# The order of all engines taken from a simulation with queues, with another opening of the first FFN

## The chip, the cores and the metric

The kernel runs on one core of one Trainium2 chip. The metric is the device time of one execution in microseconds (us). The kernel before takes 2179.03 us (median of 3 runs, 2178.09 to 2179.07). A core has TensorE (PE) for matmuls, VectorE (DVE), ScalarE (ACT) and GpSimd (POOL), and SyncE (SP), which here only issues transfers. Each engine executes its own list of instructions in order and waits on semaphores for the others.

## The reference, cut to what matters

528 tokens (16 meta tokens and 512 of the input) of 1024 channels go through two layers, each an FFN, a mixer and an FFN:

```python
def swiglu(x, w_gate, w_up, w_down):
    return (jax.nn.silu(x @ w_gate) * (x @ w_up)) @ w_down
...
def mixer(z, w_in, gla_w2, gla_b2, gla_gn, q_norm, k_norm, w_pa, w_pb, b_merge, w_out, cos, sin):
    h = z @ w_in
    (q_a, k_a, v_a, r_a, lr_f, lr_b, q_b, k_b, v_b, g_a, g_b) = jnp.split(h, SPLIT_POINTS, axis=-1)
    a = gla_branch(q_a, k_a, v_a, r_a, lr_f, lr_b, gla_w2, gla_b2, gla_gn)
    b = attention_branch(q_b, k_b, v_b, q_norm, k_norm, cos, sin)
    y = (jax.nn.sigmoid(g_a + b_merge[0]) * (a @ w_pa)
         + jax.nn.sigmoid(g_b + b_merge[1]) * (b @ w_pb))
    return y @ w_out
...
    for l in range(DEPTH):
        h = h + 0.5 * swiglu(rmsnorm(h, norm_gains[l, 0]),
                             ffn_w_gate[l, 0], ffn_w_up[l, 0], ffn_w_down[l, 0])
        h = h + mixer(rmsnorm(h, norm_gains[l, 1]), w_in[l], gla_w2[l], gla_b2[l], gla_gn[l],
                      q_norm[l], k_norm[l], w_pa[l], w_pb[l], b_merge[l], w_out[l], cos, sin)
        h = h + 0.5 * swiglu(rmsnorm(h, norm_gains[l, 2]),
                             ffn_w_gate[l, 1], ffn_w_up[l, 1], ffn_w_down[l, 1])
```

All is float32. The attention has 8 query heads of 64 on 2 key heads and runs in blocks of 128 queries.

## The kernel before, in words

Activations lie with channels on the 128 partitions and tokens along the free axis; `h` holds all eight chunks of 128 channels. Every float32 product is made of three matmuls on operands that are split into a high part (a cast, on ACT: L337 for weights, tile `whi`) and a low part (a subtraction, on DVE: L338, tile `wlo`): high by high, high by low, low by high.

**FFN.** The weights come in slabs of 128 x 1024. The products run in a scheme with seven products of half blocks instead of eight, so sums of weight blocks are needed besides the blocks. They are made by `begin_sums` and `sums`: by transfers that add into a tile (issued on POOL's queue, L255), by a negation on ACT (L250) or by a subtraction on DVE (L300). `ffn_steps` lists an FFN's steps in the order of the program: `P` is one of the seven products of a pair of FFN chunks, `S` one of the down products, `D` a plain down product, `H` the hidden values. The first FFN of the program (f = (0, 0)) opens with plain products (`G`, `F`, by `whole_matmuls`, L744), because the weights arrive while it runs; `Q` squares `h`, `R` makes the means over the channels (L523) and the reciprocal roots, and `X` makes the differences of halves of `h` that the seven products use (`differences`, L589 on ACT and L592 to L595 on DVE) and their split parts (`parts_of`, L601, L602). `early` and `late` with `direct` (L559, L560) make the split chunks of `h` that the plain products read. The loop at the end of `build` runs them with the weight pieces (L244, L245). The odd chunks' second halves come by the transfer at L1474.

**Mixer.** `project` (L517) makes one projection of 128 channels: 24 matmuls per half of the tokens. After the gated linear attention (`gla_pair`), `attention` runs over units of two blocks of 128 queries of one head: `probs` makes the scores (L1222, L1223), their maximum (DVE L1225, L1230), the exponential (ACT L496 with the read of its accumulator), the reciprocal (DVE L1232) and scales the row (ACT L1234 for the first block of a unit, DVE L1236 for the second). `weighted` transposes the probabilities (L1247, L1257), splits them (ACT L1250 and L1260, DVE L1251 and L1261) and multiplies them with the values (L1263 to L1265); the sum of both parts goes to tile `e` (ACT L1270, DVE L1271). The scores lie in tile `ss` (two buffers of two PSUM banks), transposes and weighted values in `sm` (two buffers), projections in `mm` (two buffers). The projections of the merge gates are written in part ahead of the attention and in part behind it (`gate_pairs`); what comes before what on an engine is not the order of the program alone.

**What sets the order.** The program is a list of instructions with dependencies through tiles. The scheduler of the tile framework puts them in an order for each engine, by a simulation of its own and by priorities: the program's order, `tc.high_priority()`, and `tc.issue_after(x)`, which lets an instruction become ready only behind x. On the chip each engine follows its list; a matmul that waits holds up every matmul behind it.

## Time and profile before

| | |
|---|---|
| median of 3 runs | 2179.03 us (2178.09 to 2179.07) |
| profiled execution | 2179.76 us |
| its span, first to last instruction | 2178.0 us |
| granted TensorE clock, mean | 0.998 |
| PE busy | 2152.3 us, 99% |
| DVE busy | 1795.3 us, 82% |
| ACT busy | 1238.8 us, 57% |
| POOL busy | 113.8 us, 5% |
| share of the chain that ended last | PE 81%, DVE 12%, ACT 4%, issue 2%, DMA 1% |

In the rows that the prediction shows, `<-` stands between what an instruction writes and what it reads; `xc` are operands of an FFN, `x` of the mixer, `t` scratch tiles, `q` split probabilities, `sc` scalars of a softmax row, `g` gates and FFN operands. A row of the waits has the engine, tile and line that waited, what it waited for, and the total, the times and the longest in us. A row of the groups has, behind the bar, busy us and mean ns of one instruction, then the idle us before it and what ended them. A row of the timeline has start, duration, and in brackets the idle time before it. In the rows of windows each engine has its busy us and its instructions; then come the granted clock, the DMA share and GB/s.

### The profile page before, as it was taken

To read this page: it belongs to the slowest core of one execution; us is meant where nothing else is said; L and a number is where in the kernel's file an instruction comes from. 1 tells how busy PE (TensorE), PEld (TensorE's weight loads), DVE (VectorE), ACT (ScalarE), POOL (GpSimd) and SP (SyncE) were. 2 spreads that over 40 slices of the span, in tenths; PEclk is the share of its full clock that TensorE was granted. 3 is DMA by queue.
4 is the path that set the end of the run, shared out by engine and by line. 5 is a ranking of instruction groups with operands and counts; after the bars stand their busy time and mean duration, and the time that the engine had idled before them with its cause. 6 is when DMAs were issued, how large, how long until landed. Compare 5 with 4: busy or idle time off the path is not lost.

```text
span 2178.0 us, 40250 instructions
## 1 busy us (share of the span) xinstructions
PE 2152.3 (99%) x16496; PEld 2062.5 (95%) x16496; DVE 1795.3 (82%) x2748; ACT 1238.8 (57%) x1839; POOL 113.8 (5%) x135
## 2 busy tenths in 40 slices
PE   9999999999999999999999999999999999999998
PEld 9999999989999999999999999988788888999997
DVE  7987979777976689888799879797779767997986
ACT  7645557455784556464575455574557836554544
POOL 1100000000000000010010000000000001000100
PEclk9999999999999999999999999999999999999999
DMA  7866755112113557675567667552121146775751
GB/s 219 214 178 184 211 153 143 67 59 69 49 40 126 136 169 190 194 189 179 173 164 188 195 182 204 152 138 97 49 78 50 49 136 157 201 202 177 199 160 68
DMA packets 90999, 315.08 MB, mean 145 GB/s; under 512 B 10048, under 2 KB 14016, under 8 KB 90816
## 3 DMA queue, kind: packets, MB, share of 16 engines
q1 hardware_dynamic: 70656, 244.87, 32.7%
q0 software_dynamic: 18608, 65.54, 16.9%
q8 instruction: 130, 2.13, 0.4%
q10 hardware_dynamic: 1552, 2.11, 0.3%
q14 instruction: 53, 0.43, 0.1%
HBM read 291.51 MB, written 2.10 MB: 135 GB/s over the span
## 4 chain that ended last, share of the span: by engine, by line
PE 81%; DVE 12%; ACT 4%; issue 2%; DMA 1%; ACTq 0%; DVEq 0%
PE ss L694 36%; PE mm L517 14%; PE ss L845 13%; PE ss L517 7%; DVE wlo L338 3%; PE sm L517 2%; DVE h L853 1%; DMA w<-win 1%; PE sm L1247 1%; PE ss L744 1%; DVE g L806 1%; PE ss L1222 1%; PE ss L523 1%; ACT t L496 1%; PE sm L1263 1%
## 5 line engine op out<-in xcount | busy, mean ns | idle before, releaser
L694 PE MATMUL ss<-xc,whi 128*128 128x264 f32 (+1 forms) x4704 | 858.1, 284 | 2.3 <-DVE g L781 1.0
L694 PEld LDWEIGHTS ss<-xc,whi 128*128 128x128 f32 x4704 | 726.8, 188 | 4.0 <-DVE g L781 1.2
L694 PE MATMUL ss<-xc,wlo 128*128 128x264 f32 (+1 forms) x2352 | 666.0, 283 | 1.2 <-DVE wlo L338 1.2
L338 DVE TENSOR_TENSOR wlo<-w,whi 128x1024 fp32r<-128x1024 f32 (+1 forms) x350 | 419.7, 1205 | 64.0 <-ACT whi L337 63.6
L337 ACT CAST whi<-w 128x1024 fp32r<-128x1024 f32 (+1 forms) x350 | 358.0, 1038 | 167.3 <-PE ss L694 75.5
L694 PEld LDWEIGHTS ss<-xc,wlo 128*128 128x128 f32 x2352 | 442.9, 188 | 1.8 <-DVE wlo L338 1.8
L517 PE MATMUL mm<-x,whi 128*128 128x264 f32 (+1 forms) x1712 | 385.0, 315 | 0.0
L517 PEld LDWEIGHTS mm<-x,whi 128*128 128x128 f32 x1712 | 277.8, 188 | 16.0 <-issue 1.0
L845 PE MATMUL ss<-g,whi 128*128 128x264 f32 (+1 forms) x1520 | 284.0, 285 | 4.0 <-DVE h L853 1.7
L517 PE MATMUL mm<-x,wlo 128*128 128x264 f32 (+1 forms) x856 | 265.9, 315 | 0.0
L845 PEld LDWEIGHTS ss<-g,whi 128*128 128x128 f32 x1520 | 236.1, 188 | 8.1 <-DVE g L806 4.2
L845 PE MATMUL ss<-g,wlo 128*128 128x264 f32 (+1 forms) x760 | 214.9, 283 | 0.0
L698 ACT COPY c<-ss 128x528 f32<-128x528 f32 (+1 forms) x126 | 75.0, 595 | 224.0 <-PE ss L694 223.8
L337 ACT CAST whi<-raw 128x1024 fp32r<-128x1024 f32 x114 | 119.3, 1048 | 129.2 <-PE mm L517 93.5
L338 DVE TENSOR_TENSOR wlo<-raw,whi 128x1024 fp32r<-128x1024 f32 x114 | 139.2, 1222 | 56.1 <-ACT whi L337 52.2
L517 PEld LDWEIGHTS mm<-x,wlo 128*128 128x128 f32 x856 | 159.5, 188 | 8.1 <-issue 0.5
L845 PEld LDWEIGHTS ss<-g,wlo 128*128 128x128 f32 x760 | 142.9, 188 | 0.0
L255 POOL DMA_DIRECT2D w<-win x62 | 54.4, 877 | 1475.7 <-DVE wlo L338 510.0
L496 ACT ACTIVATE c<-c 128x528 f32<-128x528 f32 (+1 forms) x88 | 56.4, 642 | 108.3 <-DVE c L771 108.2
L845 PE MATMUL ss<-c,whi 128*128 128x264 f32 (+1 forms) x608 | 115.8, 286 | 1.5 <-ACT c L803 0.7
L338 DVE TENSOR_TENSOR wlo<-s,whi 128x1024 fp32r<-128x1024 f32 (+1 forms) x90 | 107.5, 1196 | 0.9 <-ACT whi L337 0.8
L517 PE MATMUL ss<-g,whi 128*128 128x264 f32 (+2 forms) x516 | 103.7, 310 | 0.0
(295 smaller groups left out, 3536.3 us busy)
## 6 DMA issues: line engine op xcount, KB each, us to landing
w<-win SPq DMA_DIRECT2D x330, 512.0 KB, 4.3
raw<-wts SPq DMA_DIRECT2D x114, 512.0 KB, 3.3
w<-win POOLq DMA_DIRECT2D x58, 512.0 KB, 7.5
s<-win POOLq DMA_DIRECT2D x24, 512.0 KB, 7.6
w<-s POOLq DMA_DIRECT2D x24, 512.0 KB, 5.4
w<-win SPq DMA_DIRECT2D x20, 384.0 KB, 3.9
s<-w POOLq DMA_DIRECT2D x6, 512.0 KB, 8.8
h<-xt SPq DMA_DIRECT2D x3, 528.0 KB, 8.0
```

What stands on the lines that cost most here:

```text
L255: return self.nc.gpsimd.dma_start(t, src, accum_op=ALU.add)
L337: self.cast = nc.scalar.copy(hi[:, :n], w[:, :n]).ins
L338: self.low = nc.vector.tensor_tensor(lo[:, :n], w[:, :n], hi[:, :n].bitcast(F32), ALU.subtract).ins
L496: prev_act[0] = S.activation(*args, **kw).ins
L517: TE.matmul(acc.half[i][:width], lhs, rhs[:, acc.spans[i]], start=first, stop=last)
L523: TE.matmul(a, weights, x[:, hs], start=True, stop=True)
L694: closing[0] = TE.matmul(acc[:, j], a[:, j, k], b[:, at], start=bool(begin and k == 0 and i == 0), stop=k == len(x) - 1 and i == 2, skip_g ...
L698: W.behind = S.copy(part(st, q), acc).ins
L744: closing[0] = TE.matmul(acc[:, j], a[:, j, k], v, start=b in "ac" and k == 0 and i == 0, stop=b in "bd" and k == len(x) - 1 and i == 2).ins
L806: V.tensor_tensor(lo, src[:, ks], hi.bitcast(F32), ALU.subtract)
L845: closing[0] = TE.matmul(acc[:, j], a[:, j, k], xs[b][:, k], start=bool(begin and k == 0 and i == 0), stop=k == n - 1 and i == 2, skip_gro ...
L853: V.tensor_tensor(to, to, acc, ALU.add)
```

## The change

It has four parts.

1. `TileContext` gets `schedule_with_timeline_sim=True`: the scheduler orders all engines, in the whole program, by its simulation with queues. No matmul is added or removed.
2. In the opening of the first FFN the step `X 0` (differences and parts) stands ahead of the products `F 1,5`, and the means (`R`) behind them: 24 matmuls later. A new step `B` behind the means begins the sums of pair 3, whose negation is bound behind the last activation (`prev_act`) instead of at the fetch of its block.
3. Two fourth sums (of the down operations 11 and 12 of the first FFN, `early_fourth`) are made by a negation on ACT and an adding transfer on POOL's queue instead of a subtraction on DVE.
4. The eight scalings of `h` (on DVE, between products of pairs 2 and 3 of the first FFN) are spread over other products.

```diff
-            steps += [("Q", 1)] + [("F", 1, u) for u in range(2, 5)] + [("R",), ("X", 0)] + [("F", 1, u) for u in range(5, 8)]
+            steps += [("Q", 1)] + [("F", 1, u) for u in range(2, 5)] + [("X", 0), ("F", 1, 5), ("R",), ("B",)] + [("F", 1, u) for u in (6, 7)]
...
+    def early_fourth(self, f, i):
+        return f == (0, 0) and NPAIR <= i < NPAIR + QUADS
+
-    def begin_sums(self, f, i, w):
+    def begin_sums(self, f, i, w, behind=None):
...
         if self.chained(f, i):
-            s3 = self.negative(f, i, "s3", w)
+            with self.tc.issue_after(behind) if behind else nullcontext():
+                s3 = self.negative(f, i, "s3", w)
...
         elif product == "2":
             self.kept = w
+            if self.early_fourth(f, i):
+                got[f, i, "3"] = self.negative(f, i, "s4", w)
...
+        elif product == "6" and self.early_fourth(f, i):
+            self.add(got[f, i, "3"], w)
         elif product == "6":
...
-            if load[2] == "1":
+            if load[2] == "1" and load[:2] != ((0, 0), 3):
                 self.begin_sums(*load[:2], self.raws[s])
...
-                if step[1] in (2, 3) and step[2] in ("6574" if not norm.raw else "65743" if step[1] == 2 else "176"):
+                if step[1] in (2, 3) and step[2] in ("6574" if not norm.raw else "126574" if step[1] == 2 else "12"):
...
+            elif step[0] == "B":
+                W.fetch(W.at[(l, f), 3, "1"] + 1)
+                W.begin_sums((l, f), 3, W.raws[W.at[(l, f), 3, "1"]], prev_act[0])
...
-    with tile.TileContext(nc) as tc, ExitStack() as ctx:
+    with tile.TileContext(nc, schedule_with_timeline_sim=True) as tc, ExitStack() as ctx:
```

The diff shifts lines: L338 is L346 in the changed file, L560 is L568, L592 to L594 are L600 to L602, L517 is L525, L1222 and L1223 are L1233 and L1234, L1247 is L1258, L1257 is L1268, L1250 is L1261, L496 is L504, L1260 is L1271, L1234 is L1245, L1270 is L1281. The texts use the old numbers.

DVE in the opening, before, from the last piece of the second weight block on: `xc` are operands of the plain products, `wlo2` the low part of the third weight block, `g45` a tile of differences.

```order
19 L245 TENSOR_TENSOR wlo1_122<-whole1_120,whi1_121 128x256
20 L560 SCALAR_TENSOR_TENSOR xc4_133<-h_82,par_83,xc3_132 128x264
21 L560 SCALAR_TENSOR_TENSOR xc7_144<-h_82,par_83,xc6_143 128x264
22 L560 SCALAR_TENSOR_TENSOR xc9_154<-h_82,par_83,xc8_153 128x264
23 L560 SCALAR_TENSOR_TENSOR xc12_165<-h_82,par_83,xc11_164 128x264
24 L338 TENSOR_TENSOR wlo2_207<-w12_00_0_175,whi2_206 128x1024
```

The same place in the changed kernel; `g41` to `g44` are the differences.

```order
19 L245 TENSOR_TENSOR wlo1_122<-whole1_120,whi1_121 128x256
20 L600 TENSOR_TENSOR g41_618<-g41_618 128x264
21 L600 TENSOR_TENSOR g42_626<-g42_626 128x264
22 L601 SCALAR_TENSOR_TENSOR g41_618<-h_82,minus_90,g41_618 128x264
23 L602 SCALAR_TENSOR_TENSOR g41_618<-h_82,par_83,g41_618 128x264
...
35 L568 SCALAR_TENSOR_TENSOR xc12_165<-h_82,par_83,xc11_164 128x264
36 L601 SCALAR_TENSOR_TENSOR g44_642<-h_82,minus_90,g44_642 128x264
37 L602 SCALAR_TENSOR_TENSOR g44_642<-h_82,par_83,g44_642 128x264
38 L346 TENSOR_TENSOR wlo2_207<-w12_00_0_175,whi2_206 128x1024
```

Fourteen instructions of the differences have moved ahead of `wlo2`, which was the 24th and is the 38th.

PE in the attention of layer 0, before, from the transposes of one unit (`sm627`) to those of the next (`sm638`); `mm698` is a projection of a merge gate.

```order
4696 L1247 MATMUL sm627_7219<-const_84,t609_7146 128x128
4697 L517 MATMUL mm698_7856<-x181_4305,whi142_7623 128x264
4698 L1257 MATMUL sm630_7228<-const_84,t606_7134 64x128
4699 L1257 MATMUL sm630_7228<-const_84,t609_7146 64x128
4700 L517 MATMUL mm698_7856<-x180_4304,wlo142_7624 128x264
4701 L517 MATMUL mm698_7856<-x183_4312,whi142_7623 128x264
...
4709 L517 MATMUL mm698_7856<-x189_4328,whi143_7682 128x264
4710 L1247 MATMUL sm638_7269<-const_84,t620_7193 128x128
```

The same place in the changed kernel; `ss660` are the scores of a later block.

```order
4915 L1258 MATMUL sm627_7221<-const_84,t609_7148 128x128
4916 L1268 MATMUL sm630_7230<-const_84,t606_7136 64x128
4917 L1268 MATMUL sm630_7230<-const_84,t609_7148 64x128
4918 L1233 MATMUL ss660_7365<-k451_6485,qm453_6491 64x264
4919 L1234 MATMUL ss660_7365<-k452_6486,qm453_6491 64x264
4920 L1233 MATMUL ss660_7365<-k451_6485,qm453_6491 64x264
4921 L1234 MATMUL ss660_7365<-k452_6486,qm453_6491 64x264
4922 L1258 MATMUL sm638_7271<-const_84,t620_7195 128x128
```

No projection stands between these units any more. All units from `sm532` (row 4722) to `sm638` (row 4922) together have 12 rows of projections, and in layer 1 those from `sm1392` (row 12154) to `sm1521` (row 12442) have 12 too; the others of the gates stand earlier.

ACT in the changed kernel, for one such unit of layer 1:

```order
1426 L504 ACTIVATE t1500_19752,sc1499_19750<-ss1498_19745,sc1499_19750,rq1362_19182 128x528
1427 L1271 CAST lr1483_19672<-sm1482_19669 64x256
1428 L504 ACTIVATE t1503_19764,sc1502_19762<-ss1501_19757,sc1502_19762,rq1362_19182 128x528
1429 L1245 ACTIVATE t1500_19752<-t1500_19752,sc1499_19750 128x528
1430 L1261 CAST q1491_19715<-sm1490_19710 128x512
1431 L1281 COPY e1365_19195<-sm1482_19669 64x256
1432 L1261 CAST q1494_19724<-sm1493_19719 128x512
1433 L504 ACTIVATE t1514_19811,sc1513_19809<-ss1512_19804,sc1513_19809,rq1362_19182 128x528
```

Between the unit's two casts (L1250 of before) stands the copy of the last unit's values, whose tile `sm1482` shares its buffer with `sm1493`.

## The prediction

> **What bounds the kernel now.** I read the page's busy times first, then the list of waits, then windows over the attention, since the change reorders everything and the question is which engine has slack where.
>
> ```profile
> span 2178.0 us, 40250 instructions
> PE 2152.3 (99%) x16496; PEld 2062.5 (95%) x16496; DVE 1795.3 (82%) x2748; ACT 1238.8 (57%) x1839; POOL 113.8 (5%) x135
> ```
>
> PE is idle for 2178.0 - 2152.3 = 25.7 us in all. A new order adds and removes no matmul, so it can save no more than a part of that, and it can lose any amount. The waits of PE, longest groups first (us in total, times, longest):
>
> ```profile
> PE ss L845 <- DVE h L853: 1.7, 4, 0.6
> PE ss L1018 <- DVE p L1014: 1.5, 4, 0.9
> ...
> PE ss L1222 <- ACT t L496: 0.7, 3, 0.3
> ```
>
> No group is over 1.7 us, and the 17 groups of the list add up to about 15 us; leaving out the start, the opening and the tail, I put 8 us of it to the two mixers and to the seams between FFN groups. The attention of layer 0 and a piece of layer 1's, busy us of PE, PEld, DVE, ACT, POOL:
>
> ```profile
> 537.00:655.00 118.00, 116.95 (x926) 110.73 (x924) 96.92 (x236) 97.19 (x210) 0.00 (x0) 1.00 0.13 41
> ...
> 1680.00:1720.00 40.00, 39.79 (x254) 32.32 (x253) 34.70 (x85) 33.05 (x70) 0.00 (x0) 1.00 0.12 40
> ```
>
> Here PE is full although DVE and ACT are at 82 to 87%. It is full because the gate projections (L517, which nothing needs before the merge) are dealt out between the steps of the softmax. So the attention is the place where an order can cost most.
>
> **The change: the attention.** I call a unit what one step of the attention's loop issues: two score products (8 matmuls, L1222/1223), ten transposes (L1247/1257), nine weighted products (L1263 to L1265), 27 matmuls. Their pace, and that of the projections:
>
> ```profile
> 1693.54 0.62 PE L517 MATMUL mm<-x,whi 128*128 128x512 f32 x2
> 1694.00 0.39 PE L517 MATMUL mm<-x,wlo 128*128 128x512 f32 x1
> ...
> 1695.38 0.28 PE L1264 MATMUL sm<-q,k 128*128 128x256 f32 x1
> ...
> 1696.19 0.28 PE L1265 MATMUL sm<-lr,vm 128*128 128x256 f32 x1
> ...
> 1698.05 0.64 PE L1247 MATMUL sm<-const,t 128*128 128x128 f32 x4
> ```
>
> Seven starts between 1695.38 and 1696.19 make 0.116 us each; I take 0.12, so a unit is 27 x 0.12 = 3.24 us of PE. A projection matmul of 512 columns takes (1694.00 - 1693.54) / 2 = 0.23 us, and one of 264 columns about 0.12. In the old order every unit has projections in it. The new order puts them far earlier and runs out. Layer 0: from sm532 to sm638 PE's order has 200 rows, 12 of them projections; the other 188 are 7 units, of which one is the small block of 64 queries, so I count 6.5. PE's work there is 200 x 0.12 = 24.0 us. Layer 1: from sm1392 to sm1521 there are 288 rows, 12 of them projections: 9.5 units and 276 x 0.12 + 12 x 0.23 = 35.9 us of PE. I call these units bare. What a bare unit takes is set by ACT and DVE, whose rows are (mean ns at the end of the busy part):
>
> ```profile
> L496 ACT ACTIVATE t<-ss,sc,rq 128x528 f32<-128x528 f32 x32 | 25.4, 793 | 3.3 <-DVE sc L1230 2.9
> L1250 ACT CAST q<-sm 128x512 fp32r<-128x512 f32 x32 | 18.7, 584 | 2.1 <-PE sm L1247 1.9
> L1234 ACT ACTIVATE t<-t,sc 128x528 f32<-128x528 f32 x16 | 11.8, 738 | 2.0 <-DVE sc L1232 1.8
> ...
> L496 ACT ACTIVATION_READ_ACCUMULATOR t<-ss,sc,rq 128x1 f32 x32 | 6.3, 196 | 0.0
> L1270 ACT COPY e<-sm 64x256 f32<-64x256 f32 x16 | 5.9, 369 | 3.6 <-DVE sc L1230 1.6 <-PE sm L1265 1.6
> L1260 ACT CAST lr<-sm 64x256 fp32r<-64x256 f32 x16 | 5.8, 365 | 2.1 <-PE sm L1257 2.1
> ```
>
> ```profile
> L1251 DVE TENSOR_TENSOR q<-sm,q 128x512 fp32r<-128x512 f32 x32 | 21.8, 686 | 2.0 <-ACT q L1250 1.6
> L1225 DVE TENSOR_REDUCE sc<-ss 128x1 f32<-128x528 f32 x30 | 20.6, 699 | 4.0 <-PE ss L1223 3.7
> ...
> L1236 DVE TENSOR_SCALAR t<-t,sc 128x528 f32<-128x528 f32 x16 | 7.9, 493 | 0.1
> L1261 DVE TENSOR_TENSOR lr<-sm,lr 64x256 fp32r<-64x256 f32 x16 | 6.7, 418 | 0.9 <-ACT lr L1260 0.4
> L1271 DVE TENSOR_TENSOR e<-sm,e 64x256 f32<-64x256 f32 x16 | 6.6, 414 | 3.3 <-ACT e L1270 3.1
> ...
> L1232 DVE RECIPROCAL sc<-sc 128x1 f32<-128x1 f32 x32 | 5.0, 160 | 2.9 <-ACT t L496 2.5
> L1230 DVE TENSOR_TENSOR sc<-sc,rq 128x1 f32<-128x1 f32 x32 | 4.7, 150 | 0.2
> ```
>
> ACT has per unit 2 x 0.793 + 2 x 0.196 + 2 x 0.584 + 0.738 + 0.369 + 0.365 = 4.62 us; DVE 2 x (0.686 + 0.699 + 0.160 + 0.150) + 0.493 + 0.418 + 0.414 = 4.72 us. Both are above PE's 3.24, so PE must stand in a bare unit. To ACT's 4.62 comes one wait that its order forces: it runs L1250, L1270, L1250, the exponentials and L1234, and the second L1250 needs transposes that may only go into a PSUM buffer (sm has two) which L1271 has just left free: 0.41 for L1271 and 0.64 for the four transposes, 1.05 us. That makes 5.67. The old order's unit is as long, though PE was full in it:
>
> ```profile
> 1693.56 0.37 ACT L1260 CAST lr<-sm 64x256 fp32r<-64x256 f32 x1
> ...
> 1698.73 0.59 ACT L1250 CAST q<-sm 128x512 fp32r<-128x512 f32 x1 [0.79 <-PE sm L1247]
> 1699.21 0.37 ACT L1260 CAST lr<-sm 64x256 fp32r<-64x256 f32 x1
> ```
>
> I take the 5.65 between the two L1260. Layer 0 then loses 6.5 x 5.65 - 24.0 = 12.7 us, layer 1 9.5 x 5.65 - 35.9 = 17.8. Behind these stretches a few projections follow in one block, and then two units per layer without score products; I estimate 3 us of standing for these four, from the 1.05 us wait above less PE's other work. Together +33.5. The same projections, put earlier, give chains there more cover: of the 8 us of waits I let 5 go (bounds 0 and 8).
>
> **The change: the opening.** The differences of h (L589, L592 to L595) now stand ahead of the second slots (L559/560) and of the third weight block (L337, L338) on ACT and DVE.
>
> ```profile
> 12.61 1.74 ACT L559 ACTIVATE xc<-h,par 128x264 fp32r<-128x264 f32 x4
> 14.25 1.03 ACT L337 CAST whi<-w 128x1024 fp32r<-128x1024 f32 x1
> ...
> 19.34 1.99 ACT L589 ACTIVATE g<-h,par 128x528 f32<-128x528 f32 x3
> ```
>
> ```profile
> 13.24 1.70 DVE L560 SCALAR_TENSOR_TENSOR xc<-h,par,xc 128x264 fp32r<-128x264 f32 x4
> 15.31 1.23 DVE L338 TENSOR_TENSOR wlo<-w,whi 128x1024 fp32r<-128x1024 f32 x1 [0.37 <-ACT whi L337]
> ```
>
> On ACT four L589 at 0.66 go in ahead, so the cast ends at 15.3 + 2.65 = 17.9. On DVE sixteen small rows stand between the arrival of h's odd second halves and L338. That transfer was issued at 6.3 and took 8.0 us to land:
>
> ```profile
> L1474 SPq DMA_DIRECT2D h<-xt x1: 556/556/556, 6.3 to 6.3; - x1
> ...
> DMA to landing us min/median/max: 8.0/8.0/8.0
> ```
>
> 14.3 + 16 x 0.425 (1.70 / 4) gives 21.1, and L338 ends near 22.2. PE came to that block's first matmuls at 17.61 before:
>
> ```profile
> 17.61 0.41 PE L744 MATMUL ss<-xc,whi 128*128 128x264 f32 x2
> ```
>
> In its new order about six matmuls of 0.12 can go ahead of the first that reads L338's result, so it wants it near 18.3 and stands some 3.7 us. Given back are waits of the old opening, since the means (L523) come 24 matmuls later and the fourth sums of the first down group leave DVE:
>
> ```profile
> 45.04 1.13 PE L523 MATMUL ss<-t,const 128*128 128x264 f32 x4 [0.91 <-ACT whi L337]
> ...
> 61.49 0.51 PE L694 MATMUL ss<-xc,whi 128*128 128x264 f32 x2 [0.67 <-ACT c L698]
> ```
>
> 0.91 goes, of 0.67 perhaps half, and of the waits at the first down group about 1. Net +1.5 us (bounds 0 and +3.7). The two fourth sums moved from DVE to a negation on ACT and an accumulating transfer cost ACT about 2 x 1.03, the price of the cast of the same tile, and POOL's queue two transfers more; ACT is at 57% and the sums are used several products later, so I cost them at nothing. If that cover were gone, a product would stand for one such step, about 1 us. The earlier negation of pair 3, and the scalings of h, spread over other products, are off PE's path: nothing.
>
> **Sum.** 33.5 - 5 + 1.5 = +30.0 on the profiled run's 2179.76 (span 2178.0 and 1.8 outside it). That run is 0.7 above the median of the three, 2179.03, so I forecast 2209. A measurement of this kernel can tell 0.2%, 4.4 us, from no change.
>
> **The rivals.** (a) *DVE sets the pace*: the wait for the buffer hides and a bare unit takes DVE's 4.72: 30.7 - 24.0 + 44.8 - 35.9 = 15.6, less 3.5, +12: 2191. For it: DVE stood for only a few us in the old windows. Against: L1270 shows waits for PE and DVE already. (b) *The whole chain adds up*: the score pair has two buffers too, so that L1225 and L1230 (0.85) stand in line with the exponential and a unit takes 6.5: 42.3 - 24.0 + 61.8 - 35.9 = 44.2, with 4 for the last units and less 3.5, +45: 2224. (c) *TensorE slows down in the bare units*. At the start, before 7.2 us, matmuls come 0.22 us apart instead of 0.12:
>
> ```profile
> 5.24 0.42 PE L744 MATMUL ss<-g,whi 128*128 128x264 f32 x1
> 5.46 0.42 PE L744 MATMUL ss<-xc,wlo 128*128 128x264 f32 x1
> ```
>
> If the stands brought that pace back, the four transposes would take 0.44 longer and a unit 6.1: 39.7 - 24.0 + 58.0 - 35.9 + 3 - 3.5 = +37: 2216. The Trainium skill, page "TensorE: Matmul & The Clock Gate", section "A second HAM failure mode: psum-queue depth-cycling", describes short idling between groups of matmuls that does this; another part of that page asks for an idle window of about 3.4 us first. No row of the old kernel has PE standing that often; a bare unit's stands add to 2.4 us, in pieces near 1, so I give it little. (d) *The other side: faster*. DVE's instructions start up to 0.1 us before the last one's end; at that packing its ten per unit take about 3.8 us, and with no loss below (24.0 + 35.9) / 16 = 3.74 us a unit, the new order only removes waits: -8 + 1.5 = -6.5, 2173. It decides at 16 p - 59.9 = 3.5, p = 3.96 us a unit. Against: ACT's 4.62 and its forced wait. (e) *The new order doesn't do what it says*, the gates being spent early makes no odds and only the opening shows: +1.5, 2180.
>
> **How the numbers follow.** Forecast 0.47; (a) 0.18; (b) 0.12; (c) 0.06; (d) 0.09; (e) 0.08. Leaving out (d) and (e) leaves 0.83, so the range runs from under (a), 2187, to over (b), 2228. Slower by over 0.2%: 0.47 + 0.18 + 0.12 + 0.06 = 0.83; within 0.2%: 0.08; faster: 0.09.
>
> **What would show it.** Right: in the changed profile the waits of the score products and transposes for L496, L1250 and L1271 grow to some 30 us, PE falls to about 60% in the last third of both attentions, and 5.65 us lie between two L1260 there. The opening shows a wait of about 3.7 us on L338 before 23 us, and L523's is gone. Wrong: PE stays above 95% in both attentions, or the pace of bare units is under 4 us, or the lost time lies in the FFN.

## The result, and the profile after

The changed kernel takes 2298.51 us (median of 4, 2292.44 to 2300.8), the kernel before beside it 2178.69 (2178.09 to 2179.07): ratio 1.0545, 95% interval 1.0532 to 1.0557. It is slower, as forecast, but by 120 us and not by 30. The profiled run took 2300.8, and its span is 2299.0 us. The new lines shift the code: the old L694, L845 and L338 are now L702, L853 and L346, and the attention's lines are 8 to 11 higher.

The head of the changed kernel's page:

```profile
span 2299.0 us, 40286 instructions
PE 2191.7 (95%) x16496; PEld 2098.5 (91%) x16496; DVE 1792.0 (78%) x2746; ACT 1233.1 (54%) x1841; POOL 115.2 (5%) x137
```

The matmuls are as many as before, and DVE and ACT have nearly the same work (DVE 1792.0 us against 1795.3, ACT 1233.1 against 1238.8). PE is idle for 107.3 us instead of 25.7, and is also busy 39 us longer with the same matmuls. To see where, I cut both traces at the same matmul numbers (0, 2838, 6053, 8865, 11710, 13766, 16314: the first FFN, the first mixer, two FFNs, the second mixer, the last FFN). First the kernel before: from and to, length, busy us of PE, PEld, DVE, ACT and POOL, and behind them the granted clock.

```profile
1.50:358.10 356.60, 352.53 (x2839) 349.81 (x2840) 306.29 (x406) 203.93 (x271) 30.38 (x36) 1.00 0.68 191
358.10:760.70 402.60, 400.34 (x3218) 386.63 (x3217) 301.93 (x628) 237.80 (x451) 5.22 (x6) 1.00 0.25 80
760.70:1107.00 346.30, 344.78 (x2814) 343.27 (x2813) 294.16 (x374) 188.07 (x234) 25.37 (x29) 1.00 0.65 182
1107.00:1466.80 359.80, 357.59 (x2848) 352.05 (x2846) 322.98 (x417) 206.30 (x261) 27.05 (x31) 1.00 0.62 175
1466.80:1829.50 362.70, 360.07 (x2059) 301.10 (x2058) 275.94 (x545) 216.66 (x389) 5.12 (x6) 1.00 0.27 84
1829.50:2138.30 308.80, 306.69 (x2550) 303.16 (x2548) 266.08 (x330) 166.27 (x204) 20.22 (x24) 1.00 0.64 183
```

The same stages of the changed kernel:

```profile
1.50:378.50 377.00, 361.24 (x2838) 356.37 (x2839) 306.45 (x410) 207.75 (x277) 32.05 (x38) 0.98 0.67 185
378.50:800.00 421.50, 404.26 (x3217) 392.88 (x3216) 298.95 (x622) 234.46 (x447) 5.23 (x6) 0.97 0.24 75
800.00:1163.60 363.60, 352.44 (x2814) 348.79 (x2814) 295.17 (x375) 187.00 (x234) 25.27 (x29) 0.99 0.63 175
1163.60:1547.80 384.20, 367.33 (x2847) 360.01 (x2846) 324.69 (x420) 202.78 (x259) 26.96 (x31) 0.98 0.59 165
1547.80:1933.40 385.60, 364.64 (x2058) 307.82 (x2057) 273.78 (x540) 216.68 (x390) 5.22 (x6) 0.99 0.25 78
1933.40:2258.50 325.10, 311.61 (x2550) 306.22 (x2548) 264.86 (x330) 165.15 (x204) 20.05 (x23) 0.99 0.62 171
```

The two mixers (second and fifth row) are 18.9 and 22.9 us longer, 41.8 together. The four FFNs are 20.4, 17.3, 24.4 and 16.3 us longer, 78.4 together, and the forecast had given them nothing beyond the opening. Length less PE's busy time is PE's idle time: in the FFNs it rises from 9.9 to 57.3 us, in the mixers from 4.9 to 38.2. The rest, 31 us in the FFNs and 8.5 in the mixers, is PE busy for longer with the same matmuls.

The waits of PE in the changed kernel, longest groups first:

```profile
PE ss L1233 <- ACT t L504: 15.3, 15, 1.8
PE ss L853 <- DVE wlo L346: 13.7, 18, 1.0
PE ss L702 <- DVE wlo L346: 13.7, 8, 3.7
PE sm L1258 <- DVE q L1262: 7.9, 9, 1.8
PE ss L853 <- DVE h L861: 6.6, 8, 2.5
PE ss L853 <- ACT c L811: 5.6, 8, 0.8
PE ss L853 <- ACT g L808: 5.5, 8, 0.8
```

Before, no group was over 1.7 us. The first and fourth are the attentions', as forecast. The others are the FFNs': products that stand for the low part of a weight block (L346), for a free accumulator (L861) and for the operands of the down projection (L808, L811). Following the same matmul number through both traces, the lag is flat inside the first FFN's groups (+4.7 us from matmul 480 to 720) and steps at each seam between groups: to 8.8 at 960, from 8.9 to 14.4 between 1800 and 1980, to 20.4 at 2820. The steps lie where DVE was full in the kernel before: in windows of 40 us from 90, 220, 330, 840, 960, 1190, 1310, 1430, 1910 and 2030 us it is busy for over 39 us, and over 50 of the FFNs' 78 us are lost at the matmuls of these ten windows.

One seam in detail. PE's rows in the changed kernel, with the wait in brackets:

```profile
243.72 0.39 PE L853 MATMUL ss<-c,wlo 128*128 128x264 f32 x1 [0.69 <-DVE wlo L346]
...
246.20 0.39 PE L853 MATMUL ss<-c,whi 128*128 128x264 f32 x1 [0.75 <-ACT c L811]
247.24 0.39 PE L853 MATMUL ss<-g,whi 128*128 128x264 f32 x1 [0.65 <-ACT g L808]
248.43 0.56 PE L853 MATMUL ss<-g,wlo 128*128 128x264 f32 x1 [0.80 <-DVE wlo L346]
248.79 0.64 PE L853 MATMUL ss<-g,whi 128*128 128x264 f32 x2
249.23 0.42 PE L853 MATMUL ss<-g,wlo 128*128 128x264 f32 x1
```

DVE's rows over the same stretch:

```profile
242.11 0.43 DVE L818 TENSOR_TENSOR g<-g,g 128x264 f32<-128x264 f32 x1
242.45 1.22 DVE L346 TENSOR_TENSOR wlo<-w,whi 128x1024 fp32r<-128x1024 f32 x1
243.59 1.31 DVE L861 TENSOR_TENSOR h<-h,ss 128x528 f32<-128x528 f32 x2
244.81 1.25 DVE L814 TENSOR_TENSOR g<-g,g 128x1056 fp32r<-128x1056 f32 x1
245.98 1.25 DVE L818 TENSOR_TENSOR g<-g,g 128x1056 f32<-128x1056 f32 x1
247.15 1.22 DVE L346 TENSOR_TENSOR wlo<-w,whi 128x1024 fp32r<-128x1024 f32 x1
```

DVE has no gap here: PE stands because DVE is full and the low part that PE wants next lies behind two evictions (L861, which adds a finished product to `h`) and two operands (L814, L818). The two stands for ACT are of the same kind: from 242.68 to 245.62 it runs three casts of weights ahead of the operand that PE waits for at 246.20 (L811). In the old order DVE was as full at this place and PE did not stand. The windows of 220 to 260 us, before:

```profile
220.00:260.00 40.00, 39.98 (x326) 39.57 (x326) 39.87 (x50) 21.99 (x26) 3.46 (x4) 1.00 0.73 195
```

and after, where the program is 9 to 14 us behind:

```profile
220.00:260.00 40.00, 36.95 (x283) 35.91 (x282) 38.59 (x48) 23.29 (x29) 3.45 (x4) 0.96 0.67 170
```

So DVE is as good as full in both, and the reserve is not the same. From the end of a low part to the first matmul that reads it there were under 0.3 us for 12 of the 556 weight blocks before, and for 45 after.

The rows of PE above show one more thing: behind four short stands within 5 us matmul pairs start 0.44 us apart (248.79, 249.23) and not 0.24. The granted clock there:

```profile
248.40:252.00 3.60, 3.58 (x16) 3.58 (x17) 3.60 (x4) 0.00 (x0) 0.00 (x0) 0.53 0.40 127
```

By the trace's record of the granted clock, the changed kernel is at half clock 20 times between its start and its end, each time for 3.41 us or twice that, 85 us together. The kernel before is at full clock from 7.2 to 2171 us.

### The profile page after: what moved, and what is told of

It reads as the page before. It is cut to its first block, busy times and chain, and to the rows that moved or that the text cites. A ratio compares the mean times of both kernels' runs of the same rounds, so it can differ in the third digit from the quotient of the medians.

```text
span 2299.0 us, 40286 instructions
## 1 busy us (share of the span) xinstructions
PE 2191.7 (95%) x16496; PEld 2098.5 (91%) x16496; DVE 1792.0 (78%) x2746; ACT 1233.1 (54%) x1841; POOL 115.2 (5%) x137
## 3 DMA queue, kind: packets, MB, share of 16 engines
q0 software_dynamic: 18896, 66.59, 16.3%
## 4 chain that ended last, share of the span: by engine, by line
PE 75%; DVE 13%; issue 5%; DMA 4%; ACT 3%; POOL 0%; SPq 0%; DVEq 0%; POOLq 0%; ACTq 0%
PE ss L702 31%; PE mm L525 16%; PE ss L853 12%; PE ss L525 7%; DVE wlo L346 3%; PE sm L525 2%; DMA w<-win 2%; DVE h L861 1%; PE sm L1258 1%; DMA s<-w 1%; DVE g L818 1%; DVE g L814 1%; PE ss L1233 1%; DVE q L1262 1%; DVE sc L1236 1%
## 5 line engine op out<-in xcount | busy, mean ns | idle before, releaser
L702 PE MATMUL ss<-xc,whi 128*128 128x264 f32 (+1 forms) x4704 | 862.8, 285 | 2.0 <-ACT whi L345 2.0
L702 PEld LDWEIGHTS ss<-xc,whi 128*128 128x128 f32 x4704 | 730.0, 189 | 4.5 <-ACT whi L345 3.5
L702 PE MATMUL ss<-xc,wlo 128*128 128x264 f32 (+1 forms) x2352 | 667.8, 285 | 13.7 <-DVE wlo L346 13.7
L346 DVE TENSOR_TENSOR wlo<-w,whi 128x1024 fp32r<-128x1024 f32 (+1 forms) x350 | 418.4, 1207 | 80.2 <-ACT whi L345 80.1
L345 ACT CAST whi<-w 128x1024 fp32r<-128x1024 f32 (+1 forms) x350 | 357.7, 1039 | 202.3 <-PE ss L702 87.5
L702 PEld LDWEIGHTS ss<-xc,wlo 128*128 128x128 f32 x2352 | 444.4, 189 | 16.0 <-DVE wlo L346 15.5
L525 PE MATMUL mm<-x,whi 128*128 128x264 f32 (+1 forms) x1712 | 382.5, 316 | 3.1 <-ACT x L513 2.6
L853 PE MATMUL ss<-g,whi 128*128 128x264 f32 (+1 forms) x1520 | 296.2, 293 | 14.2 <-DVE h L861 6.6
L525 PEld LDWEIGHTS mm<-x,whi 128*128 128x128 f32 x1712 | 281.4, 191 | 24.1 <-ACT x L513 3.7
L525 PE MATMUL mm<-x,wlo 128*128 128x264 f32 (+1 forms) x856 | 265.9, 314 | 0.0
L853 PEld LDWEIGHTS ss<-g,whi 128*128 128x128 f32 x1520 | 246.0, 196 | 19.2 <-ACT g L808 7.1
L853 PE MATMUL ss<-g,wlo 128*128 128x264 f32 (+1 forms) x760 | 221.8, 293 | 6.4 <-DVE wlo L346 6.4
L346 DVE TENSOR_TENSOR wlo<-raw,whi 128x1024 fp32r<-128x1024 f32 x114 | 139.2, 1222 | 86.7 <-ACT whi L345 82.7
L345 ACT CAST whi<-raw 128x1024 fp32r<-128x1024 f32 x114 | 119.3, 1049 | 148.4 <-PE mm L525 97.7
L525 PEld LDWEIGHTS mm<-x,wlo 128*128 128x128 f32 x856 | 161.8, 191 | 8.2
L853 PEld LDWEIGHTS ss<-g,wlo 128*128 128x128 f32 x760 | 149.6, 197 | 8.0 <-DVE wlo L346 8.0
L346 DVE TENSOR_TENSOR wlo<-s,whi 128x1024 fp32r<-128x1024 f32 (+1 forms) x90 | 106.9, 1198 | 28.6 <-ACT whi L345 28.6
L853 PE MATMUL ss<-c,whi 128*128 128x264 f32 (+1 forms) x608 | 116.7, 287 | 10.3 <-ACT c L811 5.6
L861 DVE TENSOR_TENSOR h<-h,ss 128x528 f32<-128x528 f32 (+1 forms) x140 | 96.3, 699 | 32.9 <-PE ss L853 32.7
L504 ACT ACTIVATE c<-c 128x528 f32<-128x528 f32 (+1 forms) x88 | 55.6, 641 | 114.4 <-DVE c L779 114.3
```

The lines of the kernel that those rows point to most:

```text
L345: self.cast = nc.scalar.copy(hi[:, :n], w[:, :n]).ins
L346: self.low = nc.vector.tensor_tensor(lo[:, :n], w[:, :n], hi[:, :n].bitcast(F32), ALU.subtract).ins
L504: prev_act[0] = S.activation(*args, **kw).ins
L525: TE.matmul(acc.half[i][:width], lhs, rhs[:, acc.spans[i]], start=first, stop=last)
L702: closing[0] = TE.matmul(acc[:, j], a[:, j, k], b[:, at], start=bool(begin and k == 0 and i == 0), stop=k == len(x) - 1 and i == 2, skip_g ...
L853: closing[0] = TE.matmul(acc[:, j], a[:, j, k], xs[b][:, k], start=bool(begin and k == 0 and i == 0), stop=k == n - 1 and i == 2, skip_gro ...
```

## The experiments

The table holds, for each kernel, the median, the ratio with its interval, and how much longer than before the FFNs (with the end) and the mixers are in the profiled run, cut at the same matmul numbers (the end goes up to the last matmul). e13, which has fewer matmuls, is cut at the same places of its program.

| kernel | us | ratio (95%) | FFNs | mixers |
|---|---|---|---|---|
| the change | 2298.51 | 1.0545 (1.0532 to 1.0557) | +79.3 | +41.8 |
| e1 scheduler alone | 2298.64 | 1.0546 (1.0530 to 1.0562) | +86.8 | +37.3 |
| e2 opening alone | 2177.12 | 0.9990 (0.9981 to 0.9999) | -4.4 | +0.5 |
| e3 weight parts first | 2304.17 | 1.0573 (1.0554 to 1.0592) | +79.5 | +46.1 |
| e4 gates held back | 2330.23 | 1.0693 (1.0673 to 1.0712) | +77.4 | +76.0 |
| e5 product by product | 2307.85 | 1.0592 (1.0555 to 1.0629) | +85.6 | +40.0 |
| e6 gates dealt | 2346.20 | 1.0768 (1.0737 to 1.0799) | +73.5 | +93.2 |
| e7 both | 2360.97 | 1.0836 (1.0804 to 1.0867) | +89.0 | +91.3 |
| e8 three orders old | 2207.43 | 1.0131 (1.0099 to 1.0162) | +15.3 | +10.3 |
| e9 DVE and ACT old | 2325.22 | 1.0671 (1.0640 to 1.0702) | +29.6 | +114.0 |
| e10 PE old | 2319.38 | 1.0644 (1.0607 to 1.0681) | +85.6 | +56.7 |
| e11 DVE old | 2401.74 | 1.1022 (1.0990 to 1.1054) | +79.6 | +143.8 |
| e12 ACT old | 2360.27 | 1.0829 (1.0811 to 1.0847) | +72.2 | +109.0 |
| e13 before, no late gates | 2156.47 | 0.9896 (0.9881 to 0.9911) | -0.2 | -23.0 |
| e14 cheaper low parts | 2241.42 | 1.0285 (1.0268 to 1.0302) | +23.9 | +38.6 |
| e15 before, cheaper low parts | 2177.27 | 0.9990 (0.9980 to 0.9999) | -3.7 | +1.7 |

**Which half of the change.** e1 is the kernel before with one line of the change, e2 the changed kernel without it:

```
-    with tile.TileContext(nc) as tc, ExitStack() as ctx:
+    with tile.TileContext(nc, schedule_with_timeline_sim=True) as tc, ExitStack() as ctx:
```

> The kernel before, with nothing but the scheduler's order by its simulation with queues. Theory A (the order of all engines is the cause, the opening's edits are small): 2285 to 2305 us, with PE waits for DVE's and ACT's weight parts of 25 to 35 us in the FFNs and bare units in both attentions. Rival B (the edits of the opening and their sums and scalings cause a good part, by what they move on ACT and POOL's queue): 2200 to 2260 us.

> The changed kernel with the old way of ordering: the opening's edits alone. Theory A: within 5 us of the kernel before, 2174 to 2184. Rival B: 20 us or more above it.

The flag alone costs 119.7 us; the opening alone gains 1.8. Its interval, 0.9981 to 0.9999, just excludes no change, but the gain is less than the 0.2% that counts as a difference here. In its profiled run the first FFN is 4.1 us shorter (352.5 against 356.6). All else below is about the flag.

**Does one lifted priority mend the FFNs?** e3 gives the cast and the low part of each weight block the first claim in the new order:

```
+            with tc.high_priority():
...
+                self.low = nc.vector.tensor_tensor(lo[:, :n], w[:, :n], hi[:, :n].bitcast(F32), ALU.subtract).ins
```

> The changed kernel, with the cast and the subtraction of each weight slab at high priority. Theory A1 (in the FFNs the simulated order puts the weight parts so late that PE catches up with them): the 33 us that PE waits for these two in the changed kernel fall below 10 and the time falls by 30 to 45 us, to 2255 to 2270. Rival A2 (DVE and ACT are simply full at the seams between groups, and something has to be late): the waits go to the operands (g, c) and to h, and the time moves by less than 10 us.

Nothing is gained (FFNs +79.5). The down products' waits for low parts fall from 13.7 to 7.0 us, and others stand in their place. Two rows of PE's waits in e3 (its lines are one higher):

```profile
PE ss L854 <- DVE c L815: 15.7, 10, 2.3
...
PE ss L854 <- DVE wlo L347: 7.0, 10, 0.9
```

DVE's operands (L815, the old L806) are now what is late: the same time, under another name, as rival A2 had it.

**Does PE's mixing of products cost it?** At the seam the new order jumps between weight blocks (925 changes of block in PE's order, 759 before). e5 ties each FFN product behind the one before it:

```
-            for k, (xh, xl) in enumerate(x):
+            with after(closing[0]):
+                for k, (xh, xl) in enumerate(x):
```

> The changed kernel, with each FFN product's matmuls allowed only behind the last matmul of the product before it: PE's order changes from one weight slab to another 765 times instead of 925 (759 in the kernel before). Theory A3 (at the seams between groups the simulated order starts three or four products at once, so PE needs the parts of as many slabs early and stands at each): the FFNs get back most of what they lost, 45 to 80 us, 2215 to 2255. Rival A2 (what is late at the seams is late by DVE's and ACT's own new order): under 20 us comes back, 2280 or more.

PE's order is nearly as unmixed as before (765 changes), and the FFNs lose 85.6 us. The first wait of PE in e5:

```profile
PE ss L855 <- DVE c L815: 18.8, 10, 2.0
```

It is the operand that was late in e3 too (L815, the old L806). Low parts with under 0.3 us to spare are 10 here, as few as before the change, and yet the FFNs lose as much: the lateness has only moved again. PE's mixing of products was not the cause.

**Do the gates, given back to the attention, mend the mixers?** e4 holds each late gate projection behind the last weighted product of a unit; e6 cuts the projections into pieces of 24 or 12 matmuls and ties each to a unit by a list; e7 is e5 and e6 together.

```
+                for i in range(2):
+                    k = len(gates) - EARLY
+                    with after(anchors[min(k, len(anchors) - 1)] if k >= 0 else None):
+                        gates.append(project(x, None, both[:, i], n=n_out))
```

```
+TURN = [0, 0, 0, 1, 2, 2, 2] + list(range(3, 17))
...
+                with after(anchors[min(TURN[min(at + part, len(TURN) - 1)], len(anchors) - 1)]):
```

> The changed kernel, with each projection of the merge gates allowed only behind the last weighted product of one unit of the attention, so that every unit has about 24 matmuls of projections again. Theory A: the attentions get back their 35 to 39 us, 2260 to 2268, PE over 97% in both. Rival D (the units are slow by their own new order on ACT and DVE, whatever PE has to do): less than 12 us comes back.

> The changed kernel, with the late projections of the merge gates dealt out in pieces of 24 (layer 0) and 12 matmuls (layer 1) over the units of the attention, three pieces ahead of the first unit, as in the kernel before. Theory A: the mixers get back 25 to 39 us of the 35 to 39 that they lost, 2258 to 2273. Rival D (the new order of the units on ACT and DVE is slower by itself): less than 12 us comes back, 2285 or more.

> The edits of the two runs above together. If both theories hold and do not overlap: 2178 to 2215. If the FFNs' loss stays: 2255 or more.

All three are slower than the change, and it is the mixers that suffer: +76.0, +93.2, +91.3 instead of +41.8; in e7 the FFNs' loss stays as well (+89.0). e6 shows why such an edit under a simulated order is no test of the old deal: the order of the other engines shifts along. ACT, DVE and PE in layer 1's attention of e6:

```profile
1850.10 1.28 ACT L501 ACT_TABLE_LOAD   x1
...
1851.40 5.62 ACT L505 ACTIVATE g<-g,par 128x512 f32<-128x512 f32 x9
...
1858.14 0.69 DVE L1269 TENSOR_TENSOR q<-sm,q 128x512 fp32r<-128x512 f32 x1 [7.33 <-ACT q L1268]
...
1858.89 0.62 PE L1265 MATMUL sm<-const,t 128*128 128x128 f32 x2 [4.95 <-DVE q L1269]
```

ACT now runs a table load and nine sigmoids of the merge inside a unit of the softmax; DVE stands 7.33 us behind them and PE 4.95. Gates whose projections are done can have their sigmoid, and the new order of ACT puts it there. The change itself has this too: in layer 0 a table load at 694.93 us and twelve sigmoids to 703.76 stand ahead of the scaling of a softmax row. But there PE has projections beside them and is busy for 16.5 of the 18 us from 690 to 708. Theory A of e4 and e6 fell. Rival D's number came (nothing was given back), but it is not shown either, since the orders of ACT and DVE were made anew; the three runs only show that the place of the gates cannot be changed alone.

**Whose order is it?** e8 to e12 are e1 with engines held to the order of the kernel before: each instruction of a held engine is tied behind the one that stood before it there (37 of PE's, 103 of DVE's and 67 of ACT's instructions stay free in e8, 126 of ACT's in e12).

```
+            place = self.at[self.k]
+            self.k += 1
+            i = bisect.bisect_left(self.places, place)
+            before = self.made[self.places[i - 1]] if i else None
+            with self.tc.issue_after(before) if before is not None else nullcontext():
+                out = f(*args, **kw)
```

> The kernel before with the scheduler's simulation, but each instruction of PE, DVE and ACT may only follow the ones that stood ahead of it in the old order, so far as they are written earlier in the program. Of 16245 matmuls 37 are left out of the old order, of DVE's 2738 instructions 103, of ACT's 1765 67 (without this: 2516, 1008, 474). Control for the next three. If the loss lies in these three engines' orders, whatever their mechanism: 2175 to 2195. If the few that are left, or the orders of POOL and SP, matter: 2210 or more.

> The same with DVE and ACT alone in the old order (130 and 82 left out), PE as the simulation has it (1611 out of the old order). Theory A2 (the new orders of DVE and ACT are the cause: at the seams of the FFNs and in the attention they do work that can wait ahead of work that PE waits for): 2175 to 2210. Rival A3 (PE's new order, that starts products early and spends the projections, is the cause): 2260 or more. In between: both are needed.

> The same with PE alone in the old order (224 left out), DVE and ACT as the simulation has them (837 and 316 out of the old order). Theory A2: 2260 or more. Rival A3: 2175 to 2210.

> The same with DVE alone in the old order (146 left out), PE and ACT as the simulation has them (1733 and 330). If DVE's order is what matters of A2: 2180 to 2225. If ACT's is: 2250 or more.

> ACT alone is held to the order of the kernel before under the flag (126 of its instructions are left free), PE and DVE are simulated. Theory A (of the orders that no longer fit, ACT's is the one that costs the FFN): the four FFNs take about 30 us more than before instead of 79, as in the run with DVE and ACT both held, and the whole stays under 2270. Theory B (an order fits only the orders that it was simulated with, and holding any one engine alone makes it worse): the FFNs keep at least 75 us and the whole is 2310 to 2400.

With all three held, 91 of e1's 120 us come back, so most of the loss lies in these orders. The 28 us left fall between the two forecasts; they can come from the instructions that stay free or from the orders of POOL and SP, which was not taken further. e9 came out where rival A3 had it and e10 where theory A2 had it, so neither is right as it was put. With DVE and ACT held, the FFNs' loss falls from 86.8 to 29.6, and the mixers' grows to 114. PE alone gives 1.2 back in the FFNs (85.6), DVE alone 7.2 (79.6), ACT alone 14.6 (72.2, a little under the 75 that its second theory named). In the mixers every order that is old beside a simulated one is worse than all simulated ones (+56.7 to +143.8 against +37.3). The orders only fit together; in the FFNs the pair of DVE and ACT carries the loss, with PE's order simulated anew beside it.

**What in these orders costs the FFNs the time?** e14 makes DVE's work lighter in the changed kernel, e15 does the same before. Both leave out the true low parts of the weights: the tile gets other numbers, in less time.

```
-            self.low = nc.vector.tensor_tensor(lo[:, :n], w[:, :n], hi[:, :n].bitcast(F32), ALU.subtract).ins
+            self.low = nc.vector.tensor_scalar(lo[:, :n], w[:, :n], hi[:, :1].bitcast(F32), 1e-4, ALU.subtract, ALU.mult).ins
```

> The changed kernel, with the low part of each weight block made by an instruction with one tile as its source in place of two (it takes off the first column of whi and scales by 0.0001, so the low parts hold other numbers; it still waits for the cast and for the block). By the row of L1236 beside that of two sources it takes about 0.95 us instead of 1.22, so DVE has 460 x 0.27 = 125 us less. Theory A (the new order leaves DVE no reserve at the FFN's seams, and PE stands for DVE's time): the FFNs lose less than 40 us of before instead of 79 and the whole is under 2255. Theory B (the orders place instructions ahead of those that PE needs next, whatever DVE's load): the FFNs still lose 65 us or more and the whole stays above 2280.

> The same edit in the kernel before, as the measure for the other: its PE is 99% busy, so at most some 5 us can be had: 2174 to 2181 by both theories.

The row of the new low part, and the page's busy times, in e14:

```profile
L346 DVE TENSOR_SCALAR wlo<-raw,whi x114: 734/752/755, 357.3 to 2206.5; 128x1024 fp32r<-128x1024 f32 x114
```

```profile
PE 2166.7 (97%) x16496; PEld 2077.4 (93%) x16496; DVE 1556.8 (69%) x2746; ACT 1234.1 (55%) x1841; POOL 121.5 (5%) x137
```

It takes 0.75 us instead of 1.22, not the 0.95 that I had scaled from L1236's 0.493 for 528 columns: between 528 and 1024 columns a column costs 0.52 ns, where the two-source rows of the seam above (0.43 us for 264, 1.22 for 1024) give 1.04, and the rest is a fixed part. The Trainium skill, page "VectorE: DVE Perf Modes", section "Mode 2×_2P — use both read ports for one tensor", says that an instruction with a single source tile streams it through both read ports; the halved cost per column agrees with it.

DVE has 235 us less work, and the FFNs' loss falls from 79.3 to 23.9 us while the mixers' hardly moves (38.6). The seam of e14, same window as above:

```profile
220.00:260.00 40.00, 38.95 (x316) 38.31 (x315) 32.94 (x49) 21.13 (x25) 4.42 (x4) 1.00 0.73 198
```

DVE is busy for 32.9 of 40 us, PE idle for 1.05 instead of 3.05, and the clock is at 1.00; low parts that are ready with under 0.3 us to spare are 22 instead of 45, and the clock falls to half 7 times instead of 20. Under the old order the same edit gains 2.5 us (e15). That is theory A's outcome: in the FFNs the new order leaves DVE, which is full at the seams, no reserve; lighter work on it buys back some 55 us. One caution: the orders of e14 are simulated anew with the lighter instruction (PE changes weight blocks 875 times instead of 925), so load and order changed together.

**What does a bare unit cost by itself?** e13 is the kernel before, old order, with the late gate projections cut to one block of eight:

```
-        acc = product("w_in", Acc("mm", n), x, KC, by_half=True)
+        w = [W.next("w_in") for _ in range(KC)]
+        acc = product("w_in", Acc("mm", n), x[:nk], nk, by_half=True, w=w[:nk])
...
-        gate_pairs(KC - EARLY // 2)
+        gate_pairs(KC - EARLY // 2, 1)
```

> The kernel before with the old ordering; each of the twelve late gate projections of a layer is cut from 8 blocks to 1, so its gates hold one eighth of their sum, and 12 x 42 matmuls of 0.12 us (61 us) leave PE in layer 0, 12 x 21 of 0.23 (58 us) in layer 1. The units of both attentions are then nearly bare. If a bare unit takes the forecast's 5.65 us, 32 units take 181 us instead of the 226 to 232 they and the projections took, and the mixers fall by about 60 us of the 119. If it takes the 4.97 us seen in the changed kernel, they fall by about 82. If PE's own 3.24 were reached, by 119.

All three figures were too high: with 119 us less of matmuls the mixers fall by 23. Layer 0's sixteen units, from the first L1266 (553.61) to the seventeenth (662.92), take 109.3 us; with the projections between them they took 103.0 in the kernel before (548.02 to 650.98). The projections cost nothing there: they fill a chain that is no faster without them. Part of that is the clock: with PE standing between the units its mean is 0.84 over the 109.3 us, and it was 1.00 before. The window over most of layer 0's attention in e13:

```profile
574.00:650.00 76.00, 58.62 (x344) 48.77 (x344) 64.84 (x153) 57.47 (x127) 0.00 (x0) 0.86 0.15 49
```

And one unit of it on PE:

```profile
613.58 0.28 PE L1266 MATMUL sm<-lr,vm 128*128 128x64 f32 x1
...
616.01 0.39 PE L1223 MATMUL ss<-k,p 128*128 128x264 f32 x1 [0.90 <-ACT t L496]
...
620.75 0.42 PE L1265 MATMUL sm<-q,k 128*128 128x256 f32 x1
620.96 0.41 PE L1264 MATMUL sm<-q,k 128*128 128x256 f32 x1
...
622.00 0.28 PE L1266 MATMUL sm<-lr,vm 128*128 128x256 f32 x1
```

This one, which holds three score products instead of two, takes 8.4 us, with a stand of 0.90 for the exponentials and weighted products 0.21 us apart instead of 0.12; with its projections the same one took 7.0 before (604.28 to 611.28). In the old order a bare unit costs 109.3 / 16 = 6.8 us on average in layer 0 and 99.3 / 16 = 6.2 in layer 1 (1623.47 to 1722.76), in the simulated one 6.0 (next section), all with stretches at half clock in them. So the two orders are not far apart for a bare unit; what the new one lost is the filling.

## Why the prediction was wrong

**Direction and attention: right, and nearly of the right size.** The forecast was slower with 0.83, by gates that are spent early. So it is: PE is full from 540 to 640 us, and then come bare units. The row of 640 to 700 us of the changed kernel, and the two of layer 1's attention:

```profile
640.00:700.00 60.00, 49.15 (x346) 44.32 (x345) 46.09 (x111) 45.10 (x100) 0.00 (x0) 0.91 0.13 43
```

```profile
1740.00:1790.00 50.00, 43.27 (x247) 36.50 (x245) 42.05 (x91) 33.81 (x68) 0.00 (x0) 0.93 0.16 54
1790.00:1860.00 70.00, 57.90 (x355) 47.29 (x355) 51.03 (x119) 54.20 (x113) 0.86 (x1) 0.98 0.13 38
```

PE's idle time in them is 10.9, 6.7 and 12.1 us, 29.7 of the mixers' 38.2. PE falls to 82 to 87% there and not to the 60% that I named. PE's waits of the kinds that I had named come to 27.9 us (15.3 for the exponentials, 7.9 for L1262 and 4.7 for L1282) where I had some 30.

On the forecast's own stretches, sm532 to sm638 takes 41.3 us (646.65 to 687.94) and sm1392 to sm1521 takes 55.4 (1775.57 to 1830.98). That is 96.7 us for the 16 units that I had counted, 6.0 each and not 5.65, and 36.8 us over PE's 59.9 where I had 30.5. But it is made of other parts: PE is idle for 21.4 us of the 36.8, and the other 15.4 are matmuls at a slower pace (the granted clock is 0.88 and 0.95 there). So it is in part luck that the size is near.

Where the units run evenly they are shorter than forecast, 4.97 us. The 5.65 was a single interval of the old trace, whose sixteen units in layer 0 have a mean of 103.0 / 16 = 6.4. One such unit on PE:

```profile
675.35 0.66 PE L1258 MATMUL sm<-const,t 128*128 128x128 f32 x4
...
677.46 0.39 PE L1233 MATMUL ss<-k,p 128*128 128x264 f32 x1 [1.24 <-ACT t L504]
...
680.32 0.66 PE L1258 MATMUL sm<-const,t 128*128 128x128 f32 x4
```

680.32 - 675.35 = 4.97, 0.25 above DVE's 4.72 of rival (a), with one stand of 1.24 for the exponentials. The forced wait is there: ACT stands 0.88 us for the transposes ahead of its cast at 676.04, and 25.7 us in all its 29 waits of this kind. What I had sized wrongly is ACT's own work: its rows start some 0.1 us before the last one's end, so nine rows whose durations add up to 4.61 us take 3.87 of its time. For DVE I had seen this, in (d), and not for ACT.

Behind the bare units I had 3 us of standing; PE is idle for 4.4 us from 708 to 720 and for 4.8 from 1849 to 1866. And of the 5 us of waits that I let vanish nothing is seen: the mixers' idle time rose by 33.3. 41.8 against 28.5: this term was short by 13 us.

**The opening: the stand came, the sum was off.** PE stands for 0.51 and 2.83 us instead of 3.7, and each time for a cast (L345) and not for a low part:

```profile
17.76 0.80 PE L752 MATMUL ss<-xc,whi 128*128 128x264 f32 x3 [0.51 <-ACT whi L345]
21.39 1.03 PE L752 MATMUL ss<-xc,whi 128*128 128x264 f32 x3 [2.83 <-ACT whi L345]
```

The first stand is for the third weight block and the second for the fourth: of the six matmuls that the new order puts ahead of the first reader of the third block's low part, three read the fourth block, whose cast ends at 21.34. The low part itself is ready at 22.01, where the forecast had 22.2. L523's wait is gone, as forecast. But that stand belongs to the new order: with the old one (e2) PE has no such wait and the first FFN is 4.1 us shorter, and under the flag it is 7.1 us shorter with the edits than without (377.0 against e1's 384.1). The term was +1.5; the edits are worth -4 to -7 in the first FFN.

**The step that failed: "the attention is the place where an order can cost most", and nothing for the FFNs beyond the opening.** They lost 79 of the 120 us. I had read the windows over the attention only, and for the FFN the averages, DVE 82%. The row of 220 to 260 us shown above was there to be read: DVE busy for 39.87 of 40 us beside a full PE. Where DVE is full, a simulated order that puts two evictions ahead of a low part lets PE stand, and a full engine cannot catch up. Shown is that the FFNs' loss goes with the orders of DVE and ACT together (e8, e9) and with DVE's load (e14, with the caution above), and not with PE's order alone (e5, e10), one priority (e3) or the opening (e1, e2). Two things are not settled. One is why the simulation puts its orders so: no run compares its durations with the chip's one by one. The other is the part of the transfers: in the chain that ended last DMA has 4% and issue 5% instead of 1% and 2%, and no run holds the orders of POOL and SP.

**Rivals.** (a)'s pace of DVE is close to an even unit (4.72 against 4.97), but over the stretches it gives a loss of 15.6 us, and 36.8 were measured; (b) gives 44.2. (d) and (e) are out. (c), a slower TensorE, is real and comes nearest there, with 37.8 us for units of 6.1; I had given it 0.06. It goes beyond the attention, too: PE's busy time grew by 39 us for the same matmuls, three quarters of that in the FFNs. Part of it is the first matmul after each stand (0.39 us instead of 0.28), part is the half clock: 0.53 in the window of 248.4 to 252 us, 0.91 in 640 to 700, 0.86 in e13's attention. I had held against it that an idle window of about 3.4 us comes first: the Trainium skill's page "TensorE: Matmul & The Clock Gate" gives this in "What's actually happening". Here stands of 0.65 to 0.80 us, four within about 5 us, were enough, and the clock was at half from 248.5 to 251.9. In the 3.41 us ahead of that, from 245.07, PE was busy for 36% of the time. That agrees with the Trainium skill, same page, section "A second HAM failure mode: psum-queue depth-cycling", on short idling between groups of matmuls. It does not agree with a window that is wholly idle as the condition.

The range ended at 2228, since no case in it had a loss in the FFNs; the prediction's last sentence named that as what would make it wrong, but gave it no chance.

## What to carry to other kernels

Before an order is changed, read windows of each stage for the engines that are full beside the one that bounds: a mean of 82% hid a VectorE that was full for 40 us at each of ten seams, and there each instruction put ahead of another is paid for by whoever waits for the other. Work that fills a chain has no price of its own: 119 us of projections were worth 23 where the softmax set the pace and PE's clock fell without them, so the question about moved work is what stands bare when it is gone. Orders of several engines fit as a set; holding one of them to a better-looking order, or lifting one group, moved the waits to other names, and none of the nine runs that tried it was faster (e3 to e7, e9 to e12).

## What the runs showed of the hardware

TensorE fell to half its pace without any long idle stretch: stands of 0.65 to 0.80 us, four within about 5 us, were followed by 3.4 us at half clock, in which matmuls of 264 columns started 0.22 us apart instead of 0.12. There are 20 such stretches in the changed kernel, and none before between the start and the end. So many short waits cost more than their sum: 81 us more idle time came with 39 us more busy time for the same matmuls.

In all 17 traces the granted clock changes only at marks 3.41 us apart. Between two marks at full clock, TensorE's busy share tells what comes next: below 40% all 111 such slots were followed by half clock, from 55 to 60% 13 of 80, above 80% 15 of 10,081. In the changed kernel two slots that count as fully busy were followed by half clock as well, from 545.4 and from 586.4 us; in both, sixteen matmuls have only 2 columns.

A one-source VectorE instruction on 1024 fp32 columns took 0.75 us where the two-source one took 1.22, and that edit, with the orders it brought along, was worth 57 us in the changed kernel, where VectorE was full at the seams without reserve, and 2.5 in the one before.
